# First expert layer: token rows fetched from memory and transposed, instead of one-hot products, from the third pair of experts on

## The chip, the cores and the metric

One core of one Trainium2 chip runs the whole program. The metric is the device time of one execution in microseconds (us). Engines: PE (TensorE matrix products), DVE (VectorE), ACT (ScalarE), POOL (GpSimd) and SP, which here only starts transfers. Every engine works through its own list of instructions in order; an instruction that waits for a semaphore holds up all that stands behind it on its engine.

## The reference, cut to what matters

The program is a two-layer block (attention, then a mixture of experts, twice) followed by four more layers. The change lies in the experts of the first layer, where 512 tokens of 1024 features go through 16 experts; each token is given to two.

```python
def moe(h, w_router, b_router, w_gate, w_up, w_down):
    scores = jax.nn.sigmoid(einsum('...d,de->...e', h, w_router))
    ... # best group of four experts, the two best in it -> gates (zero for all other experts)
    g = jnp.einsum('...d,edf->...ef', h, w_gate)
    u = jnp.einsum('...d,edf->...ef', h, w_up)
    a = jax.nn.silu(g) * u * gates[..., None]
    return jnp.einsum('...ef,efd->...d', a, w_down)
```

## The kernel before

**Slots.** Each expert has 128 slots. The router gives each token a slot number in each of its two experts (`slm`, `slot`). The slots' tokens have to stand feature by feature (128 features on the partitions, slots along the free axis) to be the stationary side of the expert's matrix products. Two experts make a pair; a pair's tokens fill one `XX` buffer (high and low part, 8 feature tiles, 256 slots).

**Gather.** `one_hots(pair)` builds eight 128x128 one-hot tiles `PP` by comparing slot numbers with a row of indices (on DVE for pair 0, on POOL for the others, L1205). `gather(pair, ft)` multiplies the tokens (`NH`, `NL`: high and low parts, tokens on the partitions) by the one-hots: eight products of 256 columns (L1233), and ACT copies the result into `XX` (L1235). There are eight such gathers for a pair, 64 products.

**Expert.** `expert_gu` does 48 products of 512 columns (gate, then up; L1267), `expert_d` of the expert before does 24 (L1299). Each float32 weight piece of 128x1024 is split into a high part on ACT (`wh`, L312) and a low part (`wl = wraw - wh`, L322); six products use one piece. An expert has eight pieces for gate and up and four for down. There are 8 buffers for raw pieces and 4 each for `wh` and `wl`.

**What sets the order.** Python code writes each engine's list. `work` is a queue of small steps; `more()` takes one from it after each 12 products, six times an expert. `queue(pair)` puts the next pair's one-hots and gathers into it as the expert before the pair begins; `more(100)` empties it at each even expert. `Stream.pump` puts the splits of a piece two to three pieces ahead of its products. Mode "split" puts `wl` on DVE; mode "both" puts it on POOL for the second half of a chunk.

**Around it.** `to_moe` ends the attention: per feature tile PE transposes, ACT copies (L1079, L1080), POOL subtracts (L1081). `gating` (DVE) makes slots and gates. `keep()` is 16 POOL instructions (L618) that write the residual. At expert 15 `fetch` computes row numbers on DVE and starts eight indirect transfers on POOL (L1381) that bring the experts' results `Yd` back by token; `combine` (L1388) adds them, and PE transposes the sum (`back`, L1436 and L1446).

## Time and profile before

| | |
|---|---|
| median of 3 runs | 2784.52 us (2784.28 to 2786.77) |
| the profiled execution | 2791.59 us, span 2789.8 us |
| busy over the span | PE 95%, DVE 68%, ACT 54%, POOL 21% |
| stretch 360 to 690 us (nearly all of the 16 experts) | PE 327.2, DVE 245.1, ACT 240.2, POOL 86.3 of 330 us; transfers 304 GB/s |

The profile is one execution; times in it are microseconds from the start of the span. The profiled execution took 7 us more than the median of the runs, so the two are not mixed: a difference is worked out from the profile and then added to the median. The timeline names an instruction by its start, its length, engine, line and tiles, with the idle time ahead of it in brackets.

### The profile page before, as it was taken

Reading aid. Unit: us, or ns where it says so; the run is one execution under the profiler, and the core shown is the slowest. Engines: PE = TensorE matmul, PEld = TensorE weight load, DVE = VectorE, ACT = ScalarE, POOL = GpSimd, SP = SyncE. Lnnn points to the kernel's source line nnn. Section 1 sums busy time; section 2 is a strip of 40 time slices with the busy share of each in tenths; the row PEclk is TensorE's granted clock in tenths of the full one; section 3 lists DMA queues with packets and bytes.
Section 4 is the critical chain, followed back from the end, with each engine's and each line's share of the span. In section 5 each row is a group of like instructions: output and inputs, shape, how many; then the busy total and the mean of one; then the engine's idle time right before and its main releaser. Section 6 shows DMA issues by size and latency. Waiting matters only on the chain.

```text
span 2789.8 us, 46740 instructions
## 1 busy us (share of the span) xinstructions
PE 2660.8 (95%) x17816; PEld 2335.3 (84%) x17816; DVE 1887.3 (68%) x3090; ACT 1501.8 (54%) x2438; POOL 575.7 (21%) x548
## 2 busy tenths in 40 slices
PE   7999999999699999979999999999989999999999
PEld 4755678888577788869899999999989899997999
DVE  3267667778646889986766566665786666576764
ACT  2255467777445777765554445444553444455543
POOL 0111242330421100013420034200431200324100
PEclk9999889999799899989999999999999999999999
DMA  7544158999366599954245553455532255542554
GB/s 291 166 151 144 53 177 314 333 325 327 144 217 221 179 336 350 360 188 153 91 131 179 157 171 107 145 174 155 177 115 65 76 180 156 189 144 69 174 174 144
DMA packets 155451, 516.31 MB, mean 185 GB/s; under 512 B 22362, under 2 KB 25658, under 8 KB 155084
## 3 DMA queue, kind: packets, MB, share of 16 engines
q1 hardware_dynamic: 151440, 500.23, 53.0%
q10 hardware_dynamic: 2628, 8.83, 0.8%
q0 software_dynamic: 1152, 4.19, 0.4%
q8 instruction: 143, 2.34, 0.3%
q14 instruction: 88, 0.72, 0.1%
HBM read 504.42 MB, written 8.76 MB: 184 GB/s over the span
## 4 chain that ended last, share of the span: by engine, by line
PE 46%; DVE 7%; ACT 2%; issue 1%; POOL 1%; DMA 0%; ACTq 0%; DVEq 0%; POOLq 0%
PE ps_mm L1813 39%; DVE wl L322 2%; DVE f L2601 2%; PE ps_mm L2173 1%; PE ps_s L2216 1%; DVE kS L2055 0%; PE ps_t L2881 0%; PE ps_s L2890 0%; POOL acc L1767 0%; PE ps_mm L1866 0%; PE ps_s L2350 0%; ACT B L1756 0%; PE ps_t L2199 0%; DVE B L2614 0%; PE ps_o L1799 0%
## 5 line engine op out<-in xcount | busy, mean ns | idle before, releaser
L1813 PE MATMUL ps_mm<-B,wh 128*128 128x272 f32 (+1 forms) x6400 | 1217.5, 290 | 8.3 <-ACT B L1756 4.1
L322 DVE TENSOR_TENSOR wl<-wraw,wh 128x1024 fp32r<-128x1024 f32 (+2 forms) x845 | 993.0, 1202 | 125.5 <-ACT wh L312 123.7
L1813 PEld LDWEIGHTS ps_mm<-B,wh 128*128 128x128 f32 x6400 | 1008.0, 190 | 20.4 <-ACT B L1756 4.4
L312 ACT ACTIVATE wh<-wraw 128x1024 fp32r<-128x1024 f32 (+2 forms) x882 | 881.2, 1013 | 192.6 <-PE ps_mm L1813 100.4
L1813 PE MATMUL ps_mm<-B,wl 128*128 128x272 f32 (+1 forms) x3200 | 921.4, 288 | 2.4 <-DVE wl L322 2.3
L1813 PEld LDWEIGHTS ps_mm<-B,wl 128*128 128x128 f32 x3200 | 607.0, 190 | 3.1 <-DVE wl L322 3.1
L1813 PE MATMUL ps_mm<-W,wh 128*128 128x512 f32 (+1 forms) x736 | 205.6, 367 | 5.6 <-ACT W L554 3.1
L1767 POOL TENSOR_TENSOR acc<-acc,sq 128x272 f32<-128x272 f32 (+1 forms) x49 | 78.8, 1608 | 632.5 <-issue 441.2
L1813 PEld LDWEIGHTS ps_mm<-W,wh 128*128 128x128 f32 x736 | 130.6, 192 | 39.9 <-ACT W L803 4.2
L1267 PE MATMUL ps_mm<-wh,XX 128*128 128x512 f32 x512 | 161.7, 397 | 0.0
L1267 PE MATMUL ps_mm<-wh,W 128*128 128x512 f32 x512 | 160.7, 395 | 0.0
L1813 PE MATMUL ps_mm<-W,wl 128*128 128x512 f32 (+1 forms) x368 | 131.9, 358 | 0.4 <-DVE wl L322 0.4
L1898 ACT ACTIVATE B<-f 128x272 fp32r<-128x272 f32 (+1 forms) x88 | 37.7, 428 | 167.8 <-DVE f L1896 167.8
L322 POOL TENSOR_TENSOR wl<-wraw,wh 128x1024 fp32r<-128x1024 f32 x37 | 89.8, 2428 | 139.1 <-ACT wh L312 123.6
L1205 POOL TENSOR_SCALAR PP<-moec,rt_slm 128x128 fp32r<-128x128 f32 x60 | 80.6, 1359 | 177.8 <-PE ps_t L1233 177.8
L1267 PEld LDWEIGHTS ps_mm<-wh,XX 128*128 128x128 f32 x512 | 96.9, 189 | 21.7
L1267 PEld LDWEIGHTS ps_mm<-wh,W 128*128 128x128 f32 x512 | 96.2, 188 | 21.7
L1894 DVE TENSOR_TENSOR f<-ps_mm,R 128x272 f32<-128x272 f32 (+1 forms) x88 | 38.5, 437 | 109.7 <-PE ps_mm L1813 109.7
L1299 PE MATMUL ps_s<-wl,ah 128*128 128x512 f32 x256 | 101.8, 398 | 5.4 <-PEq L1489 3.2
L1267 PE MATMUL ps_mm<-wl,W 128*128 128x512 f32 x256 | 103.1, 403 | 2.2 <-DVE wl L322 2.2
L1267 PE MATMUL ps_mm<-wl,XX 128*128 128x512 f32 x256 | 103.7, 405 | 1.3 <-ACT wh L312 0.9
L1299 PE MATMUL ps_s<-wh,al 128*128 128x512 f32 x256 | 100.9, 394 | 0.2 <-DVE al L1288 0.2
(737 smaller groups left out, 3880.8 us busy)
## 6 DMA issues: line engine op xcount, KB each, us to landing
wraw<-in_moe SPq DMA_DIRECT2D x376, 512.0 KB, 6.2
wraw<-in_wgu SPq DMA_DIRECT2D x176, 512.0 KB, 4.8
wraw<-in_w_mod SPq DMA_DIRECT2D x80, 512.0 KB, 4.8
wraw<-in_fox_in SPq DMA_DIRECT2D x64, 512.0 KB, 4.1
wraw<-in_wdn SPq DMA_DIRECT2D x64, 384.0 KB, 3.2
wraw<-in_wdn SPq DMA_DIRECT2D x64, 320.0 KB, 3.6
wraw<-in_gdn_in SPq DMA_DIRECT2D x32, 512.0 KB, 3.8
wraw<-in_gla_in SPq DMA_DIRECT2D x24, 512.0 KB, 3.8
```

The source lines that it names most:

```text
L312: nc.scalar.activation(wh[:, :n], t[:, :n], AF.Copy)
L322: (nc.gpsimd if pool or mode == "both" and key[1] else nc.vector).tensor_tensor(wl[:, :n], t[:, :n], wh[:, :n], op=OP.subtract)
L1205: eng.tensor_scalar(PP[:, b, i * 128:(i + 1) * 128], iota_n, u3(slm)[:, b, 2 * pair + i:2 * pair + i + 1], None, op0=OP.is_equal)
L1267: nc.tensor.matmul(ps, A[:, k, sl], B[:, d], start=n_ == 0, stop=n_ == 23)
L1299: nc.tensor.matmul(acc[c], A[:, sl], B[:, d], start=first and n_ == 0, stop=last and n_ == 11)
L1767: eng.tensor_add(self.acc[:, :n], self.acc[:, :n], sq[:, :n])
L1813: nc.tensor.matmul(ps[:, :n], A[:, k, :], B[:, :n], start=start and i == 0, stop=stop and i == tot - 1)
L1894: nc.vector.tensor_mul(t2[:, :n], pu[:, :n], self.R[:, :n])
L1898: nc.scalar.activation(ah[q][:, r, :n], av[:, :n], AF.Copy)
L2173: nc.tensor.matmul(p[:, c0:c0 + n], qS[h % 2][:, h // 2, q0:q0 + 128], kS[h % 2][:, h // 2, k0:k0 + n], start=True, stop=False)
L2216: nc.tensor.matmul(o[half[e], c0:c1], t[:, m * 128 + 64 * e:m * 128 + 64 * e + 64], b[(h - 1 + e) % len(b)][:, d0:d0 + c1 - c0], start=b i ...
L2601: V.scalar_tensor_tensor(y, zp[:, j:j + T2], cw[:, j, base + m:base + m + 1], y, op0=OP.mult, op1=OP.add)
```

## The change

- The tokens' float32 rows are stored to memory (`hd`, 512 rows) as `to_moe` transposes them: one more transfer for each of eight feature tiles, started by ACT.
- After `gating`, `place()` computes on DVE for each token the place of its two slots in a list `tok` in memory, and POOL writes the tokens' numbers there with eight indirect transfers of 128 single values; then the list is read back.
- For pairs 2 to 7 of the first layer `rows_of` fetches an expert's 128 rows from `hd` by that list (one indirect transfer, 512 KB), and two steps `feature_major` transpose them with four PE transposes each; ACT takes the high part, DVE the low part. Two empty steps stand between fetch and transposes. Pairs 0 and 1 and the second layer are gathered as before; pair 7's one-hots are still made, since its results go back by them.
- From expert 3 on the gate and up weights have mode "both": each second `wl` piece is made on POOL.
- `PP` has two buffers, `ah` and `al` one; two pads and the constants change size.

```diff
-                p += [((f"gu{l}", e, i), ap[6 * e + i], 2048, "split", 1024) for i in range(4)]
+                p += [((f"gu{l}", e, i), ap[6 * e + i], 2048, "split" if l or e < 3 else "both", 1024) for i in range(4)]
...
             nc.scalar.activation(t, pt[:, :n], AF.Copy)
+            if nb == 4:
+                nc.scalar.dma_start(self.hd.rearrange("(b p) c -> p b c", b=4)[:, :, d], t.rearrange("p (b c) -> p b c", b=4))
...
-            PP = PPs[pair] = self.u("PP", [128, nb, 256], F32R, bufs=1 + l)
+            PP = PPs[pair] = self.u("PP", [128, nb, 256], F32R, bufs=2)
...
+        def place():
+            ov, val = w("ov"), w("val")
+            V.tensor_scalar(ov, slot, float(CAP), None, op0=OP.is_lt)
+            V.tensor_scalar(val, slot, 16.0, -2048.0, op0=OP.mult, op1=OP.add)
...
+            for i, m_ in enumerate((M1, M2)):
+                V.tensor_tensor(t16, val, m_, op=OP.mult)
+                f = w("fidx", nb)
+                V.tensor_reduce(f, e3(t16), axis=AX.X, op=OP.add)
+                V.tensor_copy(ii[i], f)
+            for i in range(2):
+                for b in range(nb):
+                    nc.gpsimd.indirect_dma_start(out=self.tok[:, :], in_=ids[:, b:b + 1], in_offset=None,
+                                                 out_offset=bass.IndirectOffsetOnAxis(ap=ii[i][:, b:b + 1], axis=0))
+            st["tok"] = self.u("rt_tok", [128, 16], I32)
+            nc.gpsimd.dma_start(st["tok"], self.tok[0:2048].rearrange("(s e) o -> s (e o)", e=16))
+
+        def rows_of(e):
+            st["X", e] = self.u("PP", [128, 1024], F32, bufs=2)
+            nc.gpsimd.indirect_dma_start(out=st["X", e], out_offset=None, in_=self.hd[:, :],
+                                         in_offset=bass.IndirectOffsetOnAxis(ap=st["tok"][:, e:e + 1], axis=0))
+
+        def feature_major(e, half):
+            px = self.ps("t")
+            X = st["X", e]
+            for i in range(4):
+                f = 4 * half + i
+                nc.tensor.transpose(px[:, i * 128:(i + 1) * 128], X[:, f * 128:(f + 1) * 128], self.ident)
+            src = px.rearrange("p (f s) -> p f s", f=4)
+            H, L = (XX[e // 2 % 2][:, a, 4 * half:4 * half + 4, e % 2 * 128:e % 2 * 128 + 128] for a in range(2))
+            nc.scalar.activation(H, src, AF.Copy)
+            V.tensor_tensor(L, src, H, op=OP.subtract)
...
+            if l == 0 and pair > 1:
+                for i in range(2):
+                    work.append(lambda i=i: rows_of(2 * pair + i))
+                for i in range(2):
+                    work.append(lambda: None)
+                for i in range(2):
+                    for half in range(2):
+                        work.append(lambda i=i, half=half: feature_major(2 * pair + i, half))
+                if pair == 7:
+                    work.append(lambda: one_hots(pair))
+            else:
+                work.append(lambda: one_hots(pair))
+                for ft in range(8):
+                    work.append(lambda ft=ft: gather(pair, ft))
...
         gating()
+        if l == 0:
+            place()
         self.keep()
```

Where it moves instructions, three places are shown. Lines of the changed kernel are one higher up to its L1081 (L322 is its L323), and nine higher at the one-hots (L1205 is its L1214).

First, POOL after the attention. Before, the last of `keep()` (L618) and then the one-hots of pairs 1 and 2:

```order
L618 TENSOR_SCALAR x<-W_1124,vecs 128x256 [waits DVE_49]
L618 TENSOR_SCALAR xc<-W_1124,vecs 128x256
L1397 TENSOR_LOAD rt_cnti_2739 [waits DMAHW0_49,DVE_49,DMAHW2_49,PE_49,DMAHW3_49,Activation_49,Pool_49]
L1205 TENSOR_SCALAR PP_3090<-moec,rt_slm_2734 128x128 [waits DVE_49,PE_49]
L1205 TENSOR_SCALAR PP_3090<-moec,rt_slm_2734 128x128 x7
L1205 TENSOR_SCALAR PP_3446<-moec,rt_slm_2734 128x128 [waits PE_49,Pool_49]
L1205 TENSOR_SCALAR PP_3446<-moec,rt_slm_2734 128x128 x7
```

POOL at the same place in the changed kernel, from the last subtraction of `to_moe` (L1084); L1262 is the write of token numbers into `tok`, L1265 the reading back, L619 `keep()`:

```order
L1084 TENSOR_TENSOR W_2754<-T_2921,W_2753 128x4x128 [waits Activation_49]
L1262 DMA tok<-rt_ids_2750,rt_idx_503_3055 2049x1 [waits DMAHW1_49,DVE_49,Pool_49]
L1262 DMA tok<-rt_ids_2750,rt_idx_503_3055 2049x1 [waits DMASW0_49]
L1262 DMA tok<-rt_ids_2750,rt_idx_503_3055 2049x1 [waits DMASW1_49]
L1262 DMA tok<-rt_ids_2750,rt_idx_503_3055 2049x1 [waits DMASW2_49]
L1262 DMA tok<-rt_ids_2750,rt_idx_504_3056 2049x1 [waits DMASW3_49,DVE_49]
L1262 DMA tok<-rt_ids_2750,rt_idx_504_3056 2049x1 [waits DMASW4_49]
L1262 DMA tok<-rt_ids_2750,rt_idx_504_3056 2049x1 [waits DMASW5_49]
L1262 DMA tok<-rt_ids_2750,rt_idx_504_3056 2049x1 [waits DMASW6_49]
L1265 DMA rt_tok_3073<-tok 128x16 [waits DMASW7_49]
L619 TENSOR_SCALAR x<-W_1126,vecs 128x256 [waits DMAHW5_49]
L619 TENSOR_SCALAR xc<-W_1126,vecs 128x256 [waits DMAHW6_49]
```

Each of the eight writes waits for the landing of the one ahead of it (DMASW0, DMASW1, ...), since all write `tok`; the 16 instructions of `keep()` and then pair 1's one-hots stand behind the last.

Second, POOL in the last experts. Before, one-hots of pairs 5, 6 and 7 and the eight transfers of `fetch`, and nothing else:

```order
L1205 TENSOR_SCALAR PP_4703<-moec,rt_slm_2734 128x128 x8
L1205 TENSOR_SCALAR PP_5122<-moec,rt_slm_2734 128x128 x8
L1205 TENSOR_SCALAR PP_5541<-moec,rt_slm_2734 128x128 x8
L1381 DMA XX_6200<-Yd,rt_idx_727_6202 128x1024 x4
L1381 DMA W_6201<-Yd,rt_idx_728_6203 128x1024 x4
```

In the changed kernel, from the last `wl` piece of expert 13's up weights; L1214 is pair 7's one-hots, L1440 `fetch`:

```order
L323 TENSOR_TENSOR wl_5545<-wraw_5406,wh_5531 128x1024
L1214 TENSOR_SCALAR PP_5555<-moec,rt_slm_2736 128x128 x8
L323 TENSOR_TENSOR wl_5634<-wraw_5504,wh_5620 128x1024
L323 TENSOR_TENSOR wl_5691<-wraw_5547,wh_5677 128x1024
L323 TENSOR_TENSOR wl_5715<-wraw_5580,wh_5701 128x1024
L323 TENSOR_TENSOR wl_5751<-wraw_5610,wh_5737 128x1024
L323 TENSOR_TENSOR wl_5827<-wraw_5717,wh_5813 128x1024
L323 TENSOR_TENSOR wl_5856<-wraw_5753,wh_5842 128x1024
L323 TENSOR_TENSOR wl_5880<-wraw_5777,wh_5866 128x1024
L1440 DMA XX_5909<-Yd,rt_idx_719_5911 128x1024 x4
L1440 DMA W_5910<-Yd,rt_idx_720_5912 128x1024 x4
L323 TENSOR_TENSOR wl_5944<-wraw_5805,wh_5930 128x1024
```

Four `wl` pieces an expert have come to POOL; the one-hots moved from the pair's first step to its ninth, behind a piece, and the last piece of expert 15 stands behind the eight transfers of `fetch`.

Third, DVE at expert 13, where `plain` copies pair 7's one-hots (`T<-PP`). Before:

```order
L322 TENSOR_TENSOR wl_5869<-wraw_5718,wh_5855 128x1024 [waits DMAHW3_49,PE_49,Activation_49]
L1212 CAST T_5879<-PP_5541 128x512 [waits Pool_49]
L1277 TENSOR_TENSOR T_5881<-ps_mm_5820,T_5809 128x512 [waits PE_49]
L322 TENSOR_TENSOR wl_5887<-wraw_5745,wh_5867 128x1024 [waits DMAHW4_49,Activation_49]
L322 TENSOR_TENSOR wl_5899<-wraw_5757,wh_5885 128x1024 [waits DMAHW6_49,Activation_49]
```

In the changed kernel:

```order
L323 TENSOR_TENSOR wl_5578<-wraw_5437,wh_5564 128x1024 [waits DMAHW5_49,Activation_49]
L1221 CAST T_5588<-PP_5555 128x512 [waits Pool_49]
L1336 TENSOR_TENSOR T_5590<-ps_mm_5530,T_5519 128x512 [waits PE_49]
L323 TENSOR_TENSOR wl_5596<-wraw_5461,wh_5576 128x1024 [waits DMAHW6_49,Activation_49]
L323 TENSOR_TENSOR wl_5608<-wraw_5473,wh_5594 128x1024 [waits DMAHW7_49,Activation_49]
```

DVE's list is the same here; what it waits for has moved: the one-hots are now started one step ahead of the copy, where they were started nine steps ahead.

## Rows read from the trace of the kernel before

**Rows 1.** Windows view, expert stage and end: us, busy by engine, PEclk, DMA share, GB/s.

```profile
360.00:690.00 330.00, 327.16 (x1679) 276.68 (x1679) 245.06 (x241) 240.16 (x292) 86.27 (x69) 0.99 0.87 304
...
700.00:720.00 20.00, 11.29 (x42) 8.19 (x40) 10.65 (x12) 9.35 (x11) 4.11 (x4) 0.90 0.99 386
...
722.00:726.00 4.00, 4.00 (x15) 3.61 (x16) 1.60 (x6) 0.00 (x0) 0.00 (x0) 0.50 0.00 0
```

**Rows 2.** Timeline of PE: gather, products, transposes; first products of experts 6 and 10.

```profile
465.53 1.11 PE L1233 MATMUL ps_t<-PP,W 128*128 128x256 f32 x8
466.47 0.40 PE L1299 MATMUL ps_s<-wl,ah 128*128 128x512 f32 x1
466.70 0.39 PE L1299 MATMUL ps_s<-wh,al 128*128 128x512 f32 x1
...
481.44 0.60 PE L1285 MATMUL ps_t<-csts,T 128*128 128x128 f32 x4
...
494.00 0.39 PE L1267 MATMUL ps_mm<-wl,W 128*128 128x512 f32 x1
...
577.99 0.39 PE L1267 MATMUL ps_mm<-wl,W 128*128 128x512 f32 x1
```

**Rows 3.** Timelines of POOL, DVE and PE as the experts begin.

```profile
358.00 0.62 POOL L618 TENSOR_SCALAR x<-W,vecs 128x256 f32<-128x256 f32 x1
...
367.49 0.56 POOL L618 TENSOR_SCALAR xc<-W,vecs 128x256 f32<-128x256 f32 x1
369.09 7.21 POOL L1205 TENSOR_SCALAR PP<-moec,rt_slm 128x128 fp32r<-128x128 f32 x6 [1.03 <-PE ps_t L1233]
...
361.38 0.38 DVE L1186 TENSOR_TENSOR rt_gates<-rt_t 128x64 f32<-128x64 f32 x1
...
377.52 0.86 PE L1233 MATMUL ps_t<-PP,W 128*128 128x256 f32 x5 [0.77 <-POOL PP L1205]
```

**Rows 4.** Timeline of DVE in `fetch`: the first instruction and the first row numbers.

```profile
689.39 0.19 DVE L1364 TENSOR_SCALAR rt_ov<-rt_slot 128x64 f32<-128x64 f32 x1
...
691.11 0.17 DVE L1377 CAST rt_idx<-rt_fidx 128x4 int32<-128x4 f32 x1
```

**Rows 5.** Timeline of POOL in `fetch`: the first and the last of eight indirect transfers.

```profile
692.23 1.84 POOL L1381 DMA_INDIRECT XX<-Yd,rt_idx  x1 [68.14 <-DMA wraw<-in_moe]
...
704.08 0.94 POOL L1381 DMA_INDIRECT W<-Yd,rt_idx  x1 [0.30 <-issue]
```

**Rows 6.** DMA queues, 695.5 to 696 us: POOL's queue with its first packets.

```profile
q0 software_dynamic: 2, 0.01, 4.0%
```

**Rows 7.** Timeline of SP: a write to memory, and the read that waits for it.

```profile
1281.95 0.34 SPq L2019 DMA_DIRECT2D fox_c<-z  x1
1283.65 0.27 SPq L2023 DMA_DIRECT2D B<-fox_c  x1
```

**Rows 8.** Instructions of L1320: starts of a transfer on ACT, ns min/median/max.

```profile
L1320 ACTq DMA_DIRECT2D Yd<-Y x14: 326/326/357, 410.2 to 682.8; - x14
```

**Rows 9.** Timelines of POOL and DVE where both work, in two stretches.

```profile
1641.56 2.41 POOL L322 TENSOR_TENSOR wl<-wraw,wh 128x1024 fp32r<-128x1024 f32 x1 [5.03 <-PE ps_t L2275]
...
1642.29 2.76 DVE L322 TENSOR_TENSOR wl<-wraw,wh 128x1024 fp32r<-128x1024 f32 x1
...
443.95 12.16 POOL L1205 TENSOR_SCALAR PP<-moec,rt_slm 128x128 fp32r<-128x128 f32 x8 [28.16 <-PE ps_t L1233]
...
447.30 4.72 DVE L322 TENSOR_TENSOR wl<-wraw,wh 128x1024 fp32r<-128x1024 f32 x4
```

**Rows 10.** Landing times of the eight transfers of L1381.

```profile
DMA to landing us min/median/max: 8.5/13.1/16.4
```

**Rows 11.** Timeline of PE at the end: expert 15's last piece, the first and the waiting `back`.

```profile
694.54 0.39 PE L1267 MATMUL ps_mm<-wl,W 128*128 128x512 f32 x1
...
714.08 0.39 PE L1436 MATMUL ps_mm<-T,PP 128*128 128x512 f32 x1
...
721.93 0.80 PE L1446 MATMUL ps_mm<-csts,XX 128*128 128x128 f32 x2 [1.83 <-DVE XX L1388]
```

More of the change, by code (lines that the diff above doesn't have):

```diff
@@ L176, in moe_consts @@
     fold = np.tile(np.eye(32, dtype=np.float32), (4, 1))
-    return np.concatenate([io, tri, base, low, fold], axis=1)
+    ids = i[:, None] + 128.0 * np.arange(4)
+    return np.concatenate([io, tri, base, low, fold, ids], axis=1).astype(np.float32)
 def fm(t):
@@ L996, in moe_alloc @@
         nc, c = self.nc, self.sb
-        self.moec = c.tile([128, 320], F32, name="moec")
-        nc.sync.dma_start(self.moec, self.a["moe_c"])
+        self.moec = c.tile([128, 352], F32, name="moec")
+        nc.sync.dma_start(self.moec[:, :324], self.a["moe_c"])
         self.tri = c.tile([128, 128], BF16, name="tri")
@@ L1168, in moe @@
                 nc.scalar.dma_start(self.Yd[YROWS:YROWS + 1, 512 * c:512 * c + 512], zr[0:1])
+            zi = self.u("rt_tok", [128, 16], I32)
+            nc.gpsimd.memset(zi, 0)
+            nc.scalar.dma_start(self.tok[0:2048].rearrange("(s e) o -> s (e o)", e=16), zi)
+            ids = self.u("rt_ids", [128, 4], I32)
+            nc.gpsimd.tensor_copy(ids, self.moec[:, 320:324])
         self.to_moe(*self.entry, route())
@@ L1235, in gather @@
             nc.scalar.activation(XX[pair % 2][:, :, ft, :], px.rearrange("p (a t) -> p a t", a=2), AF.Copy)
+        def place():
+            ov, val = w("ov"), w("val")
+            V.tensor_scalar(ov, slot, float(CAP), None, op0=OP.is_lt)
+            V.tensor_scalar(val, slot, 16.0, -2048.0, op0=OP.mult, op1=OP.add)
+            V.tensor_tensor(e3(val), e3(val), iota[:, None, 0:16].to_broadcast([128, nb, 16]), op=OP.add)
+            V.tensor_tensor(val, val, ov, op=OP.mult)
+            V.tensor_scalar(val, val, 2048.0, None, op0=OP.add)
+            ii = [self.u(f"rt_idx{i}", [128, nb], I32) for i in range(2)]
+            for i, m_ in enumerate((M1, M2)):
[23 more added lines that the diff above has]
+            V.tensor_tensor(L, src, H, op=OP.subtract)
         def queue(pair):
@@ L1239, in queue @@
                 XX.append(self.W(F32R, (128, 2, 8, 256)))
-            work.append(lambda: one_hots(pair))
-            for ft in range(8):
-                work.append(lambda ft=ft: gather(pair, ft))
+            if l == 0 and pair > 1:
[12 more added lines that the diff above has]
+                    work.append(lambda ft=ft: gather(pair, ft))
             if l == 1 or pair == 7:
@@ L1285, in expert_t @@
                 nc.tensor.transpose(pt[:, i * 128:(i + 1) * 128], av[:, i * 128:(i + 1) * 128], self.ident)
-            ah, al = (self.u(nm, [128, 512], F32R, bufs=2 - l) for nm in ("ah", "al"))
+            ah, al = (self.u(nm, [128, 512], F32R) for nm in ("ah", "al"))
             nc.scalar.activation(ah, pt, AF.Copy)
@@ L1310, in down @@
                     if e == 14:
-                        tiles = [self.u(t, [128, 2, 512], F32R) for t in ("Y", "PP")]
+                        tiles = [self.u(t, [128, 2, 512], F32R, bufs=n) for t, n in (("Y", 1), ("PP", 2))]
                     else:
@@ L1399, in moe @@
         if not l:
-            self.u("offset2", [128, 8], F32)
+            self.u("offset2", [128, 24], F32)
         pend, split = None, []
@@ L3150, in run @@
                 self.Yd = dr.tile([YROWS + 1, 1024], F32, name="Yd")
+                self.hd = dr.tile([512, 1024], F32, name="hd")
+                self.tok = dr.tile([2049, 1], I32, name="tok")
                 with tc.tile_pool(name="sb1", bufs=1) as self.sb:
```

## The prediction

> **What bounds the kernel now.** I read first the windows over the expert stage. From 360 to 690 us PE is busy 327.2 of 330 us at a granted clock of 0.99, DVE 245, ACT 240, POOL 86, and transfers run at 304 GB/s with a share of 0.87 [rows 1]. So PE is the bound there: a microsecond taken from its list is worth one until something else binds. The next bound is near: from 700 to 720 us the transfers ran at 386 GB/s with a share of 0.99 [rows 1]. The timeline of PE gives the prices: a gather of eight products 0.94 us (465.53 to 466.47), one 512-column product 0.23 us (466.47 to 466.70), one expert 21.0 us ((577.99 - 494.00) / 4) [rows 2]. The start and the end of the stage have limits of their own, so they are costed apart. The profiled execution lies 7 us above the median of the runs; I work out differences and add them to 2784.5.
>
> **(a) PE's list, pairs 2 to 7.** Removed for a pair: 8 x 0.94 = 7.5 us. Added: four steps of four transposes; a row of four is 0.60 us long, of which 0.40 - 0.23 = 0.17 is the tail that the next work overlaps, so 0.43 each, 1.7 us a pair [rows 2]. Net 5.8 us a pair, 2.9 an expert: PE alone would go from 21.0 to 18.1 us, and six pairs would give 35 us.
>
> **(b) The writes into `tok`, ahead of everything.** Before, POOL does `keep()` from 358.00 to 368.05, then pair 1's one-hots from 369.09 to 377.5, and PE's first gather of pair 1 already waits for them at 377.52 [rows 3]. POOL has no slack here. After, eight writes stand in front of `keep()`, each waiting until the one ahead of it has landed. The gates are ready at 361.38 + 0.38 [rows 3]; `place()` then takes DVE about what the like chain in `fetch` took, 689.39 to 691.28 = 1.9 us [rows 4]. So the first write can start at 363.4, plus a delay A. With L the time from one write's start to the next one's, pair 1's one-hots are ready at 363.4 + A + 8L + 1 (start of the read-back) + 10.05 (`keep()`) + 8.4 (one-hots) = 382.9 + A + 8L, against 377.5: a shift of 5.4 + A + 8L, and PE has only the rest of expert 0's first pieces to do meanwhile, as its list is in order.
>
> No row shows an indirect write followed by one that waits for it. Bounds of L: from above, POOL's first indirect transfer starts at 692.23 [rows 5] and its queue shows its first two packets only between 695.5 and 696 [rows 6], 3.3 to 3.8 us later; with some 0.7 us for landing and signal, 4.5. From below, SP's plain write at 1281.95 is followed by its dependent read at 1283.65, 1.70 us, of which 0.34 is SP's own start [rows 7]; with POOL's 0.94 [rows 5] in its place, 2.3. I take 3.5, nearer the upper end, since that row is of the same kind of transfer on the same queue. A: the eight `hd` stores cost ACT 0.33 us each [rows 8], in `to_moe`, whose tile takes 1.7 us of several engines; 0 to 0.3 of each is not hidden, so 0 to 2.4, taken 1.5. Together 5.4 + 1.5 + 28 = **+34.9** (5.4 + 18.4 = 23.8 to 5.4 + 2.4 + 36 = 43.8).
>
> The Trainium skill, "DMA: Bandwidth & Descriptors", section "Anatomy of one DMA — SWDGE (gpsimd) path", gives a fixed cost of about 2.0 us for each DMA that GpSimd starts. With 2.0 for L the sum would be 12 us lower; the 3.3 us to first packets in the row above speak for more.
>
> After the wait PE starts at a low clock: in the trace it had waited for most of 714 to 722 us, and from 722 to 726 the granted clock was 0.50, its lower level of 1.2 GHz [rows 1]. Four such us cost 2: **+2** (0 to 5, as the waits in (d) and (e) can do the same).
>
> **(c) Each second gate/up `wl` on POOL.** POOL takes 2.41 us for a piece, DVE about 1.2, and they hinder each other: DVE's piece started at 1642.29, beside POOL's of 1641.56, took 2.76 and ended at 1645.05, 1.08 after POOL's end at 1643.97. POOL's one-hots (one input, not two) did not do this: from 443.95 to 456.11 they ran beside four DVE pieces that took 4.72, 1.18 each [rows 9]. I therefore take the two-input pieces of the two engines as running one after the other. An expert has four on POOL and eight on DVE: 4 x 2.4 + 8 x 1.2 = 19.3 us when nothing overlaps, 18.3 if a held piece ends 1.08 after POOL's; DVE's five other steps of 0.7 lengthen it a little. This splitting chain, 19.5 us an expert (18.6 to 20.3), replaces PE's 18.1 as the pace. Transfers give nearly the same: an expert pair needs 24 weight pieces, two sets of `Yd` and two of rows, 28 x 0.52 = 14.7 MB, at 386 GB/s [rows 1] 38.0 us, 19.0 an expert. Experts 3 to 13 save 11 x (21.0 - 19.5) = **-16.5**; expert 2, still all on DVE, saves **-2.9**; experts 14 and 15, which have POOL pieces but no gathers fewer, lose **+1** (0 to 3).
>
> The fetched rows themselves are hidden: they are asked for ten pieces (14 to 15 us) ahead of the first transposes, and the eight like transfers of `fetch` landed after 8.5 to 16.4 us, median 13.1 [rows 10].
>
> **(d) Pair 7's one-hots.** They were made nine steps ahead. Now they are one step ahead of DVE's copy of them, on POOL behind a `wl` piece, and DVE's later `wl` pieces wait behind that copy. POOL needs 2.4 + 8 x 1.2 to 1.5 = 12 to 14.4 us, and DVE then some 2 for copy and piece: the next DVE piece is ready 14 to 16.5 us after the piece that POOL is at, where PE comes to it after 6 pieces of 1.4 to 1.55, some 9. PE stalls 5 to 7: **+6** (4 to 8).
>
> **(e) `fetch` at expert 15.** POOL is in its eight transfers from 692.23 to 705.02 [rows 5], and now the last `wl` piece of expert 15 stands behind them: ready at 705.0 + 2.4 = 707.4, where PE reached it at 694.54, 12.9 later. But PE waited at the end anyway, from 714.08 to 721.93, for `combine` [rows 11], which hangs on the same transfers and is not moved by this. So 12.9 - 7.9 = 5, with 1 more for the last `back` steps crowded behind: **+6** (3 to 9).
>
> **Nothing** for `place()` on DVE (DVE is idle after the gates; ACT's first `wh` comes later), the zeroing of `tok`, the constants and pads, and `ah`/`al` with one buffer (in PE's list the last reader stands ahead of the next writer). If DVE were not idle, its 1.9 us would add to (b). The second layer keeps its instructions.
>
> **The rivals.** *A, PE keeps the pace and the links are short.* If POOL's and DVE's pieces share their time better than [rows 9] shows, and transfers sustain the 405 GB/s that 14.7 MB in 36.2 us ask for, experts 2 to 13 take PE's 18.1 us and save 35 instead of 19.4, and 14 and 15 lose nothing. With L = 3.5 that is 34.9 + 2 - 35 + 6 + 6 = +14, 2798. The sign hangs on the link: the sum is 8L - 14, so at L = 2.3 it is +4, 2789, at the 1.7 of SP's row 2784, and from L = 1.1 (or 1.9, with (d) to (b)'s clock at their low ends) it would be faster by over 5.6 us. For it: SP's row. Against: [rows 6, 9].
>
> *B, transfers bind earlier.* If memory gives the expert stage clearly less than 386 GB/s (304 is what PE asked for before, 405 would be asked now), say 360, a pair takes 41 us, 20.5 an expert: the saving of experts 2 to 13 falls to 6, and the sum is 34.9 + 2 - 6 + 1 + 6 + 6 = +44, 2828. For it: a share of 0.87 at 304 GB/s. Against: 386 in the row of 700 to 720.
> The Trainium skill, "DMA: Bandwidth & Descriptors", section "Where 436 GB/s comes from", puts the limit of the memory for a core at about 358 GB/s; by it nearly all of the saving would go, but the row of 386 disagrees.
>
> *C, rows land late.* If they take 16.4 us under the heavier traffic, PE waits 2 us a pair, six times: +12, 2827.
>
> **How the numbers follow.** 34.9 + 2 - 16.5 - 2.9 + 1 + 6 + 6 = +30.5, so 2784.5 + 30.5 = **2815**. Low ends together (23.8 + 0 - 29.3 + 0 + 4 + 3 = +1.5) give 2786; the high ends (43.8 + 5 - 10.6 + 3 + 8 + 9 = +58) 2843, and both are unlikely at once. Chances: forecast 0.60, A 0.20 (half with L under 2.5), B 0.09, C 0.05, others 0.06. Range 2788 to 2838. A measurement of this kernel can tell about 0.2%, 5.6 us, from no change: faster 0.07, same 0.12, slower 0.81.
>
> **What would show it.** On POOL eight starts of L1262 some 3.5 us apart from about 365, and pair 1's one-hots ending near 411; PE waiting over 30 us at its first gather of pair 1. An expert at 19.5 us, with PE no longer full, DVE pieces of up to 2.8 us beside POOL's. A PE wait of some 6 us in expert 13 and of 13 before the last piece of expert 15, and no wait for `combine`. I am wrong if POOL issues the eight writes in under 20 us, if PE stays full at 18.1, or if the transposes wait for their rows.

## The result, and the profile after

| | before | after |
|---|---|---|
| median of the runs | 2784.63 us | 2838.68 us (2837.59 to 2841.18) |
| ratio, with its 95% interval | 1 | 1.0181 (1.0166 to 1.0197) |
| profiled execution's span | 2789.8 us | 2839.4 us |
| a pair of experts, middle of the stage | 42.0 us | 42.7 us |

The ratio is not the quotient of these two medians, which is 1.0194; that lies inside its interval.

The changed kernel is slower by 54 us in the medians, 49.6 in the profiled executions. The forecast was +30.5, with a range to 2838; the median lies 0.7 us above that end, and 2784.5 times the ratio, 2834.9, inside it. The sign and four of the five parts came out near their terms. One did not: the experts were to run at 19.5 us each and run at 21.3.

To see where the time went, I compare the two profiles at marks that both have. The handiest is `ah` (ACT, L1287 before, L1346 after), which comes once an expert. Its shift against the kernel before:

| stretch | shift at its end, us | change within, us | forecast, us |
|---|---|---|---|
| start, to the `ah` of expert 0 | +33.4 | +33.4 | +36.9 |
| to expert 2 | +29.2 | -4.2 | -2.9 |
| to expert 12 | +32.5 | +3.3 | some -15 |
| expert 13 (pair 7's one-hots) | +40.7 | +8.2 | +4.5 |
| expert 14 | +42.4 | +1.7 | +0.5 |
| to the first L635 after `back` (expert 15, `fetch`, end) | +46.8 | +4.4 | +6.5 |

(Parts (b) and its clock make the forecast's first line; -16.5 over eleven experts, +6 and +1 are spread over the others.) The remaining 2.8 us of the span came later, in stages with the same instructions; no run here looks into them.

**Start.** The timeline of POOL in the changed kernel (start, length, engine, line, tiles, idle time ahead): the first four and the last of the eight writes, the reading back, the first of `keep()`, pair 1's one-hots. They answer to POOL's in [rows 3].

```profile
367.69 1.24 POOL L1262 DMA_INDIRECT tok<-rt_ids,rt_idx  x1 [5.92 <-issue]
371.85 0.97 POOL L1262 DMA_INDIRECT tok<-rt_ids,rt_idx  x1 [2.92 <-DMA tok<-rt_ids,rt_idx]
374.26 1.74 POOL L1262 DMA_INDIRECT tok<-rt_ids,rt_idx  x1 [1.44 <-DMA tok<-rt_ids,rt_idx]
381.03 0.95 POOL L1262 DMA_INDIRECT tok<-rt_ids,rt_idx  x1 [5.03 <-DMA tok<-rt_ids,rt_idx]
...
394.29 0.95 POOL L1262 DMA_INDIRECT tok<-rt_ids,rt_idx  x1 [1.51 <-DMA tok<-rt_ids,rt_idx]
396.71 0.59 POOL L1265 DMA_DIRECT2D rt_tok<-tok  x1 [1.47 <-DMA tok<-rt_ids,rt_idx]
397.35 0.56 POOL L619 TENSOR_SCALAR x<-W,vecs 128x256 f32<-128x256 f32 x1
...
405.93 4.67 POOL L1214 TENSOR_SCALAR PP<-moec,rt_slm 128x128 fp32r<-128x128 f32 x8
```

Each write waits for the landing of the one ahead of it, as the releaser in the brackets says. From the first start to the reading back are 29.0 us, on average 3.63 a link (from one start to the next). The links are not alike: 4.16, 2.41, 6.77, 4.26, 4.01, 2.53, 2.46 and 2.42 us. The longest stood beside transfers of 166 GB/s; the last three had next to none beside them (share 0.01), but so had the one of 4.01, which no run explains. PE at the same place:

```profile
407.19 0.58 PE L1242 MATMUL ps_t<-PP,W 128*128 128x256 f32 x1 [29.55 <-POOL PP L1214]
```

PE waits 29.55 us for the one-hots that stand behind all this. In the kernel before that wait was 0.77 [rows 3]. Of the shift of 33.4 us, 1.7 was there before the first store to `hd` (ACT's first copy of `to_moe` starts at 345.08 in place of 343.38). Executions differ by as much: in e4_before_both, which has none of the writes and stores, ACT was 4.5 us later at about that place.

**The experts.** Windows of 440 to 680 us (busy time of PE, PE's weight load, DVE, ACT and POOL, then granted clock, DMA share, GB/s), of before and then of after:

```profile
440.00:680.00 240.00, 240.00 (x1229) 202.23 (x1228) 187.53 (x180) 178.88 (x216) 60.80 (x40) 1.00 0.92 323
```

```profile
440.00:680.00 240.00, 215.65 (x959) 164.22 (x957) 177.49 (x152) 168.37 (x196) 134.53 (x54) 1.00 0.96 348
```

PE is no longer full, and no other engine is: DVE 177, ACT 168, POOL 135 of 240. A kernel in which nothing is full is held by a chain of waits. Waits in the same stretch, after (engine, who waited, for what: us in total, times, longest), the four that matter:

```profile
POOL wl L323 <- ACT wh L313: 103.1, 27, 17.5
...
ACT wh L313 <- PE ps_mm L1326: 28.2, 31, 2.1
PE ps_mm L1326 <- POOL wl L323: 22.8, 32, 1.4
...
PE ps_mm L1326 <- DVE wl L323: 1.5, 5, 0.3
```

PE waits for POOL's pieces; POOL is idle until ACT has made their `wh`; ACT is idle until PE is through an earlier piece. Read as a ring, PE to ACT to POOL to PE, it names the suspect, and DVE's pieces are hardly in it. The pieces themselves (groups by line; after the bar busy time and mean ns of one):

```profile
L323 DVE TENSOR_TENSOR wl<-wraw,wh 128x1024 fp32r<-128x1024 f32 x95 | 145.1, 1553 | 9.9 <-ACT wh L313 9.6
L323 POOL TENSOR_TENSOR wl<-wraw,wh 128x1024 fp32r<-128x1024 f32 x43 | 119.3, 2776 | 103.3 <-ACT wh L313 103.1
```

Both are longer than alone (1.2 and 2.4 us, [rows 9]): they do hinder each other.

**The end.** `ah` of experts 12 to 15, then POOL and DVE at expert 13, PE there, and PE at expert 15's last piece, all of after:

```profile
683.07 0.60 ACT L1346 ACTIVATE ah<-ps_t 128x512 fp32r<-128x512 f32 x1
711.57 0.59 ACT L1346 ACTIVATE ah<-ps_t 128x512 fp32r<-128x512 f32 x1
730.51 0.59 ACT L1346 ACTIVATE ah<-ps_t 128x512 fp32r<-128x512 f32 x1
757.20 0.60 ACT L1346 ACTIVATE ah<-ps_t 128x512 fp32r<-128x512 f32 x1 [3.54 <-PE ps_s L1358]
```

```profile
687.76 6.88 POOL L1214 TENSOR_SCALAR PP<-moec,rt_slm 128x128 fp32r<-128x128 f32 x8
...
693.90 0.59 DVE L1221 COPY T<-PP 128x512 f32<-128x512 f32 x1 [3.91 <-POOL PP L1214]
...
698.08 0.80 PE L1358 MATMUL ps_s<-wl,ah 128*128 128x512 f32 x1 [5.87 <-DVE wl L323]
```

```profile
735.39 0.79 PE L1326 MATMUL ps_mm<-wl,W 128*128 128x512 f32 x1 [2.07 <-DVE wl L323]
747.07 0.79 PE L1326 MATMUL ps_mm<-wl,W 128*128 128x512 f32 x1 [8.75 <-POOL wl L323]
...
764.86 4.87 DVE L1447 SCALAR_TENSOR_TENSOR XX<-W,rt_gt,XX 128x1024 f32<-128x1024 f32 x4 [0.24 <-ACT XX L1444]
```

Here are (d), 5.87 us behind the copy of the one-hots, and (e), 8.75 us behind the transfers of `fetch`. The 2.07 us are not new: there PE waits for a DVE piece that stands behind the row numbers of `fetch`, and it did so before:

```profile
693.04 0.50 PE L1267 MATMUL ps_mm<-wl,W 128*128 128x512 f32 x1 [2.17 <-DVE wl L322]
```

The last row of after answers to [rows 11]: the four steps of `combine` now follow each other without a wait, so the wait at the end is gone, as reckoned.

### The profile page after: what moved, and what is told of

It is laid out like the page before. It is cut to its first block, busy times and chain, and to the rows that moved or that the text cites. A ratio compares the mean times of both kernels' runs of the same rounds, so it can differ in the third digit from the quotient of the medians.

```text
span 2839.4 us, 46189 instructions
## 1 busy us (share of the span) xinstructions
PE 2644.6 (93%) x17528; PEld 2298.2 (81%) x17528; DVE 1886.6 (66%) x3073; ACT 1489.8 (52%) x2414; POOL 676.7 (24%) x583
## 4 chain that ended last, share of the span: by engine, by line
PE 45%; DVE 6%; ACT 1%; issue 1%; POOL 1%; DMA 0%; ACTq 0%; POOLq 0%; DVEq 0%
PE ps_mm L1874 39%; DVE f L2662 1%; DVE wl L323 1%; PE ps_mm L2234 1%; PE ps_s L2277 1%; DVE kS L2116 0%; PE ps_t L2942 0%; PE ps_s L2951 0%; POOL acc L1828 0%; PE ps_mm L1927 0%; PE ps_s L2411 0%; PE ps_t L2260 0%; PE ps_o L1860 0%; DVE yl L2284 0%; DVE B L2675 0%
## 5 line engine op out<-in xcount | busy, mean ns | idle before, releaser
L323 DVE TENSOR_TENSOR wl<-wraw,wh 128x1024 fp32r<-128x1024 f32 (+3 forms) x793 | 973.4, 1251 | 136.9 <-ACT wh L313 92.7
L323 POOL TENSOR_TENSOR wl<-wraw,wh 128x1024 fp32r<-128x1024 f32 x89 | 234.3, 2634 | 262.7 <-ACT wh L313 251.3
L1326 PE MATMUL ps_mm<-wl,XX 128*128 128x512 f32 x256 | 107.3, 419 | 15.0 <-POOL wl L323 12.9
L1358 PE MATMUL ps_s<-wh,ah 128*128 128x512 f32 x256 | 102.3, 400 | 0.0
```

The source lines that it names most:

```text
L323: (nc.gpsimd if pool or mode == "both" and key[1] else nc.vector).tensor_tensor(wl[:, :n], t[:, :n], wh[:, :n], op=OP.subtract)
L1326: nc.tensor.matmul(ps, A[:, k, sl], B[:, d], start=n_ == 0, stop=n_ == 23)
L1358: nc.tensor.matmul(acc[c], A[:, sl], B[:, d], start=first and n_ == 0, stop=last and n_ == 11)
```

## The experiments

These ten runs were made beside the kernel before, whose median there was 2787 to 2789 us; ratios are against that. The time of a pair is the distance between `ah` of expert 4 and of expert 12, by four; an expert's pace is half of it. Three accounts of the 21.3 us are set against each other: latency (PE comes for a piece before POOL has it), exclusion (the pieces of POOL and DVE hold each other up, so that the sum of their work is the pace) and transfers (memory gives no more).

| run | what it changes | median, us | ratio (95%) | a pair, us | PE's wait for POOL's `wl`, 440 to 680 |
|---|---|---|---|---|---|
| changed kernel | | 2838.7 | 1.0181 (1.0166 to 1.0197) | 42.7 | 22.8 |
| e1_split | all `wl` on DVE | 2790.8 | 1.0009 (0.9996 to 1.0021) | 37.0 | none |
| e2_late | list written later | 2821.9 | 1.0119 (1.0093 to 1.0146) | 42.6 | 23.3 |
| e3_wh5 | 5 `wh`, 7 raw buffers | 2866.0 | 1.0278 (1.0252 to 1.0305) | 43.8 | 19.7 |
| e4_before_both | kernel before with (c) | 2835.3 | 1.0164 (1.0137 to 1.0192) | 49.6 | 3.7 |
| e5_halves | half pieces on POOL | 2827.0 | 1.0143 (1.0122 to 1.0165) | 40.7 | 7.5 |
| e6_unlinked | eight lists | 2829.4 | 1.0155 (1.0134 to 1.0176) | 42.9 | 24.4 |
| e7_best | e1, eight lists, written later | 2760.4 | 0.9906 (0.9885 to 0.9927) | 37.1 | none |
| e8_dve7 | pair 7's one-hots on DVE | 2831.2 | 1.0158 (1.0138 to 1.0178) | 42.6 | 21.9 |
| e9_oneinput | POOL fills with zeros | 2885.3 | 1.0336 (1.0315 to 1.0357) | 51.2 | 41.9 |
| e10_lead | one piece more lead | 2852.3 | 1.0223 (1.0196 to 1.0249) | 41.2 | 14.7 |

### Part (c) undone

```diff
-    ... 2048, "split" if l or e < 3 else "both", 1024) ...
+    ... 2048, "split", 1024) ...
```

> The changed kernel with part (c) undone alone: every wl piece of gate and up is again made on DVE. In the changed kernel an expert takes 21.3 us (a pair 42.7), where 19.5 was forecast. Latency theory: PE gets a POOL piece too late, since wh (1.07 us on ACT) can be written only when PE has freed one of four buffers, POOL then needs 2.4 to 3.3 us, and PE comes for the piece three pieces of 1.39 us later. Without POOL's pieces the waits of PE for them (23 us between 440 and 680 us) go, DVE has 12 x 1.22 + 5 x 0.69 = 18.1 us an expert, PE 18.1: a pace of 18.3 to 19.2, about 25 us less for experts 3 to 12; (d) shrinks by about 4 and (e) by about 7: near 2802 us (2793 to 2812). Transfers theory: 343 GB/s at a share of 0.95 is what memory gives, so the pace stays at 21.3 and only (d) and (e) shrink: about 2828.

Measured 2790.8, better than the latency theory's range, and far from the transfers theory. Windows, PE's only wait and DVE's pieces of this kernel, 440 to 680 us:

```profile
440.00:680.00 240.00, 238.14 (x1107) 190.40 (x1106) 218.66 (x222) 189.04 (x219) 22.26 (x19) 1.00 1.00 388
```

```profile
PE ps_mm L1326 <- DVE wl L323: 1.8, 6, 0.3
```

```profile
L323 DVE TENSOR_TENSOR wl<-wraw,wh 128x1024 fp32r<-128x1024 f32 x154 | 180.4, 1219 | 8.3 <-ACT wh L313 8.2
```

PE is full again, and an expert takes 18.5 us; part (a), 18.1 by PE's list, was right. DVE carries all pieces with 219 of 240 us, so the help of POOL was not needed. Transfers run at 388 GB/s with a share of 1.00: rival B falls as an account of 21.3 us, and the row of 386 [rows 1] was near the limit. The Trainium skill, "DMA: Bandwidth & Descriptors", section "Where 436 GB/s comes from", has about 358 GB/s for a core, half of what two cores share; here, where one core runs, 388 held for 240 us.

So part (c) costs the changed kernel 48 us (2838.7 - 2790.8), and the rest of the change together comes to about nothing. In the profiles it is 51.1 us: by the marks of `ah`, 28.3 in experts 3 to 12 and 21.9 in experts 13 to 15, where (d) and (e) hang on POOL's pieces. PE's waits (24.3 us in 440 to 680, here 1.8) are most of what the slower pace costs in that stretch, some 32 us (5.7 a pair); no run separates the rest.

### The writes moved behind pair 1's one-hots

```diff
-        (in place(): eight indirect writes of tok, then the reading back)
...
-                work.append(lambda: one_hots(pair))
+                work.append(lambda: (one_hots(pair), write_tok()) if l == 0 and pair == 1 else one_hots(pair))
```

> The changed kernel with the eight writes of tok and its reading back moved on POOL behind keep() and pair 1's one-hots; nothing else. If (b) is what the start costs, PE's wait of 29.6 us at the first gather of pair 1 goes and the shift of 33.7 us at the end of that gather falls to 1 to 4 us (what the hd stores and place() on DVE cost): 2805 us (2802 to 2809), with the experts' pace at 21.3 unchanged. A rival, that the wait was for something else at the start (weights, slots): the time stays near 2838.

Measured 2821.9: half of what was expected. The start gave back what was expected (`ah` of expert 0 at 398.83 in place of 429.29, 30.5 us), but expert 2 took 35.0 us in place of 21.0. POOL's first and last write, reading back and first row fetch, and PE's first transposes:

```profile
380.53 1.25 POOL L1266 DMA_INDIRECT tok<-rt_ids,rt_idx  x1 [0.19 <-POOL PP L1214]
...
422.68 1.16 POOL L1266 DMA_INDIRECT tok<-rt_ids,rt_idx  x1 [4.94 <-DMA tok<-rt_ids,rt_idx]
429.92 0.60 POOL L1269 DMA_DIRECT2D rt_tok<-tok  x1 [6.09 <-DMA tok<-rt_ids,rt_idx]
434.04 1.01 POOL L1274 DMA_INDIRECT PP<-hd,rt_tok  x1 [3.52 <-DMA rt_tok<-tok]
...
438.81 1.09 PE L1283 MATMUL ps_t<-csts,PP 128*128 128x128 f32 x4 [12.24 <-DMA PP<-hd,rt_tok]
```

A link takes 6.2 us here ((429.92 - 380.53) / 8; the eight lie between 4.9 and 7.5), not 3.6: the same chain, now beside other transfers of 281 GB/s on average. It ran past the time at which pair 2 needs its rows, and PE waited 12.24 us for them. (b) is confirmed as the cost of the start; moving a chain into traffic made it longer.

### One `wh` buffer more

```diff
-    ... tag="wh", bufs=net.split_bufs)
+    ... tag="wh", bufs=5)
...
-    raw_bufs = 8
+    raw_bufs = 7
```

> The changed kernel with five wh buffers in place of four and seven raw buffers in place of eight, the same memory; for the whole program. Latency theory: wh no longer waits for PE's last release, so POOL's piece starts about 1.2 us earlier, PE's waits for POOL pieces fall to less than half of 23 us and the pace from 21.3 to 19.3 to 20.2: 10 to 20 us less in the expert stage. Transfers theory: the pace stays at 21.3, or gets worse with one raw buffer fewer. Throughput theory (the pieces of DVE and POOL exclude each other and fill the time): stays at 21.3 too. Other stages may move a few us by the ring of seven, so the pace in the profile decides, not the total.

The pace got worse, 43.8 a pair. Waits, 440 to 680 us:

```profile
PE ps_mm L1326 <- POOL wl L323: 19.7, 29, 1.4
...
ACT wh L313 <- DMA wraw<-in_moe: 9.6, 13, 1.4
```

The wait for POOL is hardly less, and with a raw buffer fewer ACT waits for weights, which it never did in this stretch of the changed kernel; PE's wait for DVE's pieces rose from 1.5 to 8.1. That the four `wh` buffers alone close the ring is not borne out; the run cannot clear them either, since it took a raw buffer away.

### Part (c) alone, on the kernel before

```diff
-    ... 2048, "split", 1024) ...
+    ... 2048, "split" if l or e < 3 else "both", 1024) ...
```

> The kernel before with part (c) alone: each second wl piece of gate and up on POOL from expert 3 on, gathers by one-hot products as before. As forecast in (c) (19.3 us of splitting against PE's 21.0): the pace stays 21.0 and only the last piece behind the transfers of fetch costs, some 6 us: 2790. Latency theory: in the steps without a gather PE comes for a piece after 4.2 us and waits for POOL there, 0.5 to 1 us an expert more: 2796 to 2805. Transfers theory: 304 GB/s were asked for, so nothing: 2790.

Measured 2835.3, 47 us slower, missed by both theories: a pair takes 49.6 in place of 42.0. PE waits little for `wl` here. POOL and PE in one pair, and the windows of 440 to 680 us, show other reasons:

```profile
559.24 2.39 POOL L322 TENSOR_TENSOR wl<-wraw,wh 128x1024 fp32r<-128x1024 f32 x1 [1.45 <-ACT wh L312]
561.60 5.61 POOL L1205 TENSOR_SCALAR PP<-moec,rt_slm 128x128 fp32r<-128x128 f32 x8
...
563.81 0.39 PE L1233 MATMUL ps_t<-PP,W 128*128 128x256 f32 x1 [0.47 <-POOL PP L1205]
```

```profile
440.00:680.00 240.00, 222.58 (x1043) 179.03 (x1042) 146.02 (x108) 151.62 (x184) 132.51 (x79) 0.95 0.80 275
```

The next pair's one-hots, which POOL used to make well ahead, now stand behind a piece, and PE comes for them while POOL is still at them (13.7 us in all in the stretch); from 565 to 570 us the granted clock was 0.72, in the whole stretch 0.95 in place of 1.00. It is (d) in every pair. How the 7.6 us a pair divide was not measured; an estimate from these numbers is 2.8 for the one-hots (13.7 x 49.6 / 240), 0.8 for the wait for `wl` (3.7 us) and up to 2.5 for the clock (0.05 x 49.6), which leaves 1.5 or more.

### Half pieces on POOL

```diff
-    (nc.gpsimd if pool or mode == "both" and key[1] else nc.vector).tensor_tensor(wl[:, :n], ...)
+    if mode == "half":
+        nc.vector.tensor_tensor(wl[:, :512], t[:, :512], wh[:, :512], op=OP.subtract)
+        nc.gpsimd.tensor_tensor(wl[:, 512:n], t[:, 512:n], wh[:, 512:n], op=OP.subtract)
...
```

> The changed kernel with POOL's share cut otherwise: from expert 3 on every wl piece of gate and up is made in halves, columns 0 to 511 on DVE and 512 to 1023 on POOL, in place of each second piece whole on POOL. POOL's and DVE's work stay the same in sum; the time from a wh to its wl falls from 2.4 to 3.3 us to some 1.3 to 1.7. Latency theory: PE's waits for POOL between 440 and 680 us fall from 23 to under 8 us and the pace from 21.3 to 18.5 to 19.3: 2803 to 2818. Exclusion theory (the two engines' two-input pieces run one after the other, so the sum of their work is the pace): 4 x 1.22 + 8 x (0.64 + 1.25) = 20 us and more, pace 20 to 21.3: 2825 to 2839.

Both theories get a part. Windows, PE's only wait and the halves:

```profile
440.00:680.00 240.00, 230.45 (x1010) 171.46 (x1009) 216.11 (x202) 176.15 (x204) 159.37 (x101) 1.00 0.97 362
```

```profile
PE ps_mm L1330 <- POOL wl L325: 7.5, 11, 0.9
```

```profile
L325 POOL TENSOR_TENSOR wl<-wraw,wh 128x512 fp32r<-128x512 f32 x88 | 144.0, 1660 | 76.5 <-ACT wh L313 76.2
L324 DVE TENSOR_TENSOR wl<-wraw,wh 128x512 fp32r<-128x512 f32 x88 | 106.3, 1236 | 9.9 <-ACT wh L313 9.9
```

With the shorter time from `wh` to `wl` PE's wait for POOL fell from 22.8 to 7.5 us, as the latency theory said, and a pair from 42.7 to 40.7. But DVE's halves, 0.67 us at the shortest, take 1.24 on average, and DVE comes to 216 of 240 us; the total, 2827, is where the exclusion theory put it. Shortening the one cost raised the other.

### POOL's piece without its second input

```diff
+    if mode == "both" and key[1] and key[0][0] == "gu0":
+        nc.gpsimd.tensor_scalar(wl[:, :n], wh[:, :n], 0.0, None, op0=OP.mult)
+        nc.gpsimd.tensor_scalar(wl[:, :256], wh[:, :256], 0.0, None, op0=OP.mult)
...
```

> The changed kernel with the subtraction left out of the pieces that POOL makes: they are filled with zeros by two instructions that read one input (wh), 128x1024 and then 128x256 again, chosen to last about as long (2.6 us) as POOL's subtractions do in the changed kernel (2.78 mean); the low part of those pieces is missing from the products. Exclusion theory (DVE's pieces 1.55 us beside POOL's, 1.22 alone): one-input work on POOL does not hold DVE up, so DVE's pieces fall to 1.2 and the pace from 21.3 to 18.5 to 19.5: 2800 to 2817. Latency theory: the time from wh to wl is the same, PE still waits for POOL's pieces (some 20 us of 240) and the pace stays at 20.7 to 21.3: 2830 to 2839. Part of each: in between.

The pieces, and the windows of 440 to 680 us:

```profile
L324 POOL TENSOR_SCALAR wl<-wh 128x1024 fp32r<-128x1024 f32 x35 | 106.8, 3050 | 77.6 <-ACT wh L313 77.4
L327 DVE TENSOR_TENSOR wl<-wraw,wh 128x1024 fp32r<-128x1024 f32 x80 | 99.4, 1263 | 21.7 <-ACT wh L313 21.2
L325 POOL TENSOR_SCALAR wl<-wh 128x256 fp32r<-128x256 f32 x34 | 40.2, 1183 | 2.8
```

```profile
440.00:680.00 240.00, 198.08 (x819) 152.43 (x818) 127.94 (x127) 142.75 (x165) 155.68 (x78) 0.92 0.84 296
```

The two fills took 4.2 us together, not the 2.6 that I had meant, so the run does not hold the latency still; it raises it. For telling the theories apart it is the better for that. DVE's pieces are back at 1.26 us: DVE is no longer held up, and the pace is not better but much worse, 51.2 a pair, with PE waiting 41.9 us for POOL. The granted clock was 0.92 here, where the changed kernel had 1.00; an estimate of what that costs is up to 4.1 of the 51.2 us (8%), so the pair stays well above 42.7 without it. The time that POOL takes over a piece sets the pace in this run, not what it takes from DVE.

Put in a row, by the time from the start of POOL's work on a piece to its end: no piece on POOL 37.0 us a pair, halves of 1.66 us 40.7, pieces of 2.78 42.7, fills of 4.23 51.2. The order is the latency theory's; the steps can't be read as a price, since the runs differ in more than this time (eight halves an expert on POOL in place of four pieces, and the clock of the last).

### More lead

```diff
-    raw_bufs = 8
-    split_bufs = 4
+    raw_bufs = 6
+    split_bufs = 5
...
-            i = min(i, max(self.used + 1, self.loaded - 5))
+            i = min(i, max(self.used + 1, self.loaded - 3))
...
+        self.ws.ahead = 4
```

> The changed kernel with wh and wl made one piece earlier in every engine's list (four and three ahead, where it was three and two, in the expert stage of both layers), five buffers each for wh and wl and six raw ones in place of eight; the same memory. Latency theory: PE comes for a POOL piece some 1.5 us later after its wh, its waits for POOL fall from 23 us to under 8 and the pace to 18.5 to 20, unless ACT then waits for raw pieces, which the trace would show as ACT waiting for a transfer. Exclusion theory: the pace stays at 21.3. The total is not the measure, since other stages have the smaller ring of raw pieces too.

Inconclusive in size, in the direction of the latency theory. Waits:

```profile
ACT wh L313 <- DMA wraw<-in_moe: 37.3, 61, 2.0
...
PE ps_mm L1326 <- POOL wl L323: 14.7, 23, 1.3
```

A piece more of lead takes PE's wait for POOL from 22.8 to 14.7 and a pair from 42.7 to 41.2, although ACT now waits 37 us for raw pieces, of which there are only six.

### Eight lists in place of one

```diff
-    nc.gpsimd.indirect_dma_start(out=self.tok[:, :], in_=ids[:, b:b + 1], ...)
+    nc.gpsimd.indirect_dma_start(out=self.toks[4 * i + b][:, :], in_=ids[:, b:b + 1], ...)
...
+        V.tensor_reduce(tf, t8.rearrange("p k e -> p e k"), axis=AX.X, op=OP.add)
```

> The changed kernel with eight lists in place of the one tok (each zeroed, written by one of the eight transfers, read back, and the eight added up on DVE before pair 2): no write waits for the landing of another; their place ahead of keep() stays. If the start costs what the chain of landings costs, eight starts of about 1.2 us and eight reads of 0.7 us with one landing between them stand ahead of keep() instead of 29 us: some 17 us, so the first gather of pair 1 ends 12 us earlier: 2827 (2823 to 2831). If POOL's transfers cost the same unlinked (the queue takes one at a time, 3.6 us each), the time stays near 2838.

Measured 2829.4. POOL's first and last write and the last reading back:

```profile
368.96 1.24 POOL L1262 DMA_INDIRECT tok<-moec,rt_idx  x1 [5.36 <-DVE rt_t L1256]
...
378.76 1.97 POOL L1262 DMA_INDIRECT tok<-moec,rt_idx  x1 [0.30 <-issue]
...
386.79 0.53 POOL L1266 DMA_DIRECT2D rt_t<-tok  x1 [0.60 <-DMA tok<-moec,rt_idx]
```

From first write to the end of the reading 18.4 us in place of 29.6; `ah` of expert 0 comes 10.2 us earlier. Without the chain of landings 11.2 of the 29.6 us go, as (b) has it, although there are seven more reads; eight starts and eight reads are what is left.

### Pair 7's one-hots on DVE

```diff
-    eng = nc.gpsimd if pair else nc.vector
+    eng = nc.gpsimd if pair % 7 else nc.vector
```

> The changed kernel with pair 7's one-hots on DVE (3.5 us for eight, as pair 0's) in place of POOL; nothing else. By (d) they cost 8 us at expert 13 because they stand on POOL behind a wl piece with DVE waiting behind them: PE's wait of 5.9 us there goes and expert 13 falls from 28.5 to 22 to 24 us: 2833 (2830 to 2836). If the wait there was for the gates or the transposes behind the copies, it stays: 2838.

Measured 2831.2; expert 13 takes 22.6 us in place of 28.5 (`ah` of experts 12 and 13):

```profile
684.16 0.60 ACT L1346 ACTIVATE ah<-ps_t 128x512 fp32r<-128x512 f32 x1
...
706.73 0.59 ACT L1346 ACTIVATE ah<-ps_t 128x512 fp32r<-128x512 f32 x1
```

Made on DVE, the one-hots no longer stand on POOL behind a piece, and 5.9 us go, as (d) has it. In e1_split, where they are still on POOL but with no piece ahead of them, expert 13 takes 19.7 us.

### What is left when all three are mended

The kernel of e1_split with the eight lists, written behind pair 1's one-hots.

> The changed kernel with (c) undone (all wl of gate and up on DVE), eight unlinked lists, and their writing moved behind keep() and pair 1's one-hots. From the run with (c) undone (2790.8) the 31 us of the start go that moving the writes gave back; the 14 us that PE lost at expert 2, where its rows came late, don't appear, since the list is there by about 400 us: 2760 (2755 to 2768), 0.9% faster than the kernel before. If the rows of pair 2 are late again, 2770 or more.

Measured 2760.4, ratio 0.9906 (0.9885 to 0.9927): 0.9% faster than the kernel before, and where it was expected. The last reading back and the first fetch of rows, and the windows of 440 to 640 us:

```profile
399.91 0.53 POOL L1270 DMA_DIRECT2D rt_t<-tok  x1 [0.79 <-DMA wraw<-in_moe]
416.70 1.25 POOL L1281 DMA_INDIRECT PP<-hd,rt_tok  x1 [16.25 <-PE ps_mm L1339]
```

```profile
440.00:640.00 200.00, 198.07 (x916) 157.90 (x915) 183.74 (x187) 157.86 (x183) 20.25 (x17) 1.00 1.00 393
```

The list is back 16 us before the first rows are asked for, and PE does not wait for rows. PE is at 198 of 200 us and the transfers at a share of 1.00, so both are at their limit here; DVE with 184 is near its own. Which of them a further change would meet first, no run shows.

## Why the prediction was right in sign and short in size

**(a)** was right: without (c) the experts run at 18.5 us against the 18.1 of PE's list.

**(b)** was right in mechanism and near in size: +34.9 and +2 for the clock, measured +33.4. The link, the term with the widest bounds (2.3 to 4.5, taken 3.5), was 3.63 us on average, and that is partly luck: with no transfers beside it a link mostly took 2.4 to 2.5, near the lower bound, and of the four longer ones (4.0 to 6.8) three stood beside other transfers, which the prediction did not reckon with. The 0.7 us for landing and signal that it added without a row came out: the packets of the writes at 389.30 and 391.83 end 0.7 to 0.8 us ahead of the next start. Two more errors cancelled: the first write started at 367.69 where 364.9 was reckoned, and pair 1's one-hots took 4.67 us, not 8.4. The gates and 1.9 us make 363.7, not 363.4, so the delay A was 4.0, outside its bounds of 0 to 2.4: the gates came 3.4 us later than before (1.7 of it ahead of `to_moe`), and `place()` took 2.3. After the wait the clock was low for about as long as reckoned: 0.50 until 412 us and 0.58 from 412 to 415, of which PE could have used the time from the last one-hots on, some 4 us from 410.65. The Trainium skill, "DMA: Bandwidth & Descriptors", section "Anatomy of one DMA — SWDGE (gpsimd) path", has about 2.0 us of fixed cost a DMA; the undisturbed links of 2.4 to 2.5 us come near that, the mean of 3.63 does not.

**(c)** is the step that failed: "This splitting chain, 19.5 us an expert (18.6 to 20.3), replaces PE's 18.1 as the pace." It added up the work of POOL and DVE and took the sum for the pace, and an expert took 21.3. That the pieces lengthen each other was right (1.55 and 2.78 us). (With held pieces ending 1.08 after POOL's, the sum is 18.8, not 18.3.) But neither engine was full; what set the pace was the time between one `wh` and its `wl`, 2.4 to 3.3 us on POOL in place of 1.2 on DVE, in an order that makes pieces only two to three ahead. e5, e9 and e10 bear that out: with shorter pieces or more lead PE waited less for POOL and the pace got better, with longer fills it got worse though DVE was no longer held up. That the exclusion has a share of its own is suggested by e5, with DVE at 216 of 240 us and 40.7 a pair in place of 37.0, but not shown. What was reckoned as a cover for DVE was not needed, and cost 48 us of the 54, (d) and (e) with it. Experts 3 to 12 lost 3 us where 15 were to be saved.

I had the lead in the text of the kernel before ("two to three pieces ahead of its products") and the duration of POOL's piece in [rows 9], and did not set the one against the other: three pieces of 1.4 us are 4.2, and 1.07 for `wh` and 2.4 for `wl` are 3.5; with the up to 3.3 that POOL took here they are 4.4. That comparison would have shown that little of the lead was left, before the sum was made, though not that it would be overrun.

What precisely closes the ring stays open. PE's wait follows POOL's time and the lead; the count of `wh` buffers alone (e3) did not mend it, but that run had a raw buffer fewer. ACT's list also ties the next `wh` to the copies between, which wait for PE. A run with more buffers of all kinds was not tried.

**(d)** was +6, measured 5.9 by e8 (8.2 in the whole of expert 13, which has the slower pace in it). **(e)** was +6, measured +4.4: PE waited 8.75 us, not 12.9, and the waits for `combine` went as reckoned.

**The rivals.** A had the right pace for PE but not for this kernel. e1 has A's pace, but no POOL pieces and so little of (d) and (e); A's 2798 without those 12 us is 2786, and e1 gave 2790.8. B fell with 388 to 394 GB/s. (By its 360 GB/s, or the 358 cited beside it, 6 of 19.4 us of saving would have stayed, so "nearly all of the saving would go" said too much.) C did not happen where the list was in time; it happened in e2_late, through the list and not through the rows.

## What to carry to other kernels

Before a step is moved to a slower engine to relieve a faster one, set its duration against the lead that the order gives it, not only its sum against the busy share: at a lead of two or three pieces, a step twice as long can be the pace while no engine is full. Writes that share one buffer in memory are a chain of landings; give each its own and add up after, and put them where nobody stands behind them on the queue. And when a change has three parts, run each undone: here two of them hid a gain of 0.9%.
